# A decoder step on one core: the decode's first queries spread on the chip, its first gathers behind a weight load, weight pages asked for earlier, and two paces of the background work

## The chip, the cores and the metric

One core of one Trainium2 chip runs one program. The metric is the device time of one execution in microseconds (us), the median of several runs. All times within an execution are counted from the first instruction of the profiled execution.

## What is computed

One inference step of a one-layer hybrid decoder for two groups that share all weights: a prompt of 1024 rows and a sample group of 8 sequences with one new row each.

```python
q, k, v, logf, u, z = mixer_inputs(rmsnorm(x, g_mix), w_in, b_f, g_sgu_v)
x = x + concat(rmsnorm(attention), rmsnorm(gated)) @ w_o
x = x + cross_attend(rmsnorm(x, g_cross), mk, mv, w_cq, w_co)
h = rmsnorm(x, g_ffn) @ w_up                  # 5632 columns
f = (silu(conv(gate)) * conv(val)) @ w_down   # causal, width 3
y = rmsnorm(x + f, g_final)
```

The prompt attends causally to its own 1024 rows. Each of the 8 sample rows attends to 64 pages of 128 rows in a paged cache (8 heads of 64, float32), that is 16 MB of keys and 16 MB of values for each sequence, read through a page table. Cross-attention has 256 memory rows; the prompt computes the keys and values, the sample reads them from a cache. Outputs are the final rows of both groups, the new keys and values, and the convolution's states.

## The kernel before

**Two streams of work in one program.** `prompt()` is the main stream. Its phases are, in this order: `p1` (the input projection in four weight blocks of w_in: q, then forget logits and u, then k and v, then z), attention over rows 0 to 511 (`att0`, `attx`), attention over rows 512 to 1023 (`att1`), and then twice, for each half of the rows, `mid` (output projection, cross-attention, its output projection) and `ffn` (44 tiles of w_up in four groups, each followed by its part of w_down). Every large product is made of three float32r matmuls: ACT rounds a weight or activation to a high part (L235, L238), DVE subtracts to get the low part (L236, L239), and PE multiplies (L272, L273, L274).

`sample()` is the background stream: `decode()` (the paged attention of the 8 sequences), then `sample_rest()` (everything after it for the 8 rows).

**How the streams are woven.** Both are generators. Each `yield` of the main stream gives a number, a rough count of PE work. The loop at the end of `build` adds it to an account; when the account reaches `PACE[phase]` it runs one step of the background, takes the pace off the account once for each unit that the step yields, and runs at most `int(t / pace) + 1` steps after one main yield. So a larger pace means fewer background steps in that phase. After `decode()` ends, the pace is `PACE['rest']`, 2.9, in every phase. While `held` is set (the end of each output projection and the norm after it) no step runs, but the account grows; while `paused` is set nothing is added. What is left of the background when the main stream ends runs after it.

The order that results is the program order. A list scheduler in the kernel builder then takes instructions by that order as a priority and by its own simulated times, so an engine's instructions can swap places where that simulation finds an older one not ready.

**decode().** 148 steps, one yield unit each (in attention phases a step with keys is cut into five yields of 0.2). Step g of the first 128 is `kstep` for sequence g // 16, chunk g % 16: an indirect DMA on POOL's queue gathers 1 MB of keys into one of four `kv` buffers (L1428), DVE multiplies them by the query row that is spread over 128 partitions (`qb`; L1444, or L1435 in attention phases) and reduces (L1448, L1436). 18 steps later `vstep` gathers 1 MB of values (L1489), two chunks at every second step, and PE multiplies them by the weights (L1495). The query row of a sequence comes from `prep(b)`: `qs_d`, a DRAM copy that `q_sample` writes (L465), is read back by a broadcasting DMA on SP's queue (L1398). `prep(0)` runs at the start of the first step, `prep(b + 1)` at chunk 14 of sequence b.

**sample_rest().** It normalizes the attention result, then calls `sample_proj` for w_o, w_cq and w_co, with a norm ahead of the next product, cross-attention over the cached memory between w_cq and w_co (8 pages of keys, 8 of values), then 11 double pages of w_up, the gated convolution, and 11 pages of w_down. Each page is 1 MB, goes into the same four `kv` buffers and is asked for on POOL's queue by `page` (L1568). `sample_proj` asks for two pages, yields 2, multiplies them (L331), asks for the next two. After the last norm the old convolution states `stT` are loaded into a `kv` buffer, weighted, and written out as `o_s1` (L1757), one yield.

**PSUM.** `BK()` hands out banks in turn: of three calls one gets a `bb` bank (two of them), two get a `ba` bank (four of them). In the first block of `p1`, `by_rows` holds four banks for tiles 0 to 3 until ACT scales them out (L469), which needs `rstd8` (L412 on POOL).

Of the kernel before, what the change touches and what calls it, by code (L numbers as in the profile page):

```python
# [18 lines left out]
P = 128  # L19
# [53 lines left out]
KS = 2  # L73
BKQ = 1
LA = (2, 2)
PACE = {'p1': 7.0, 'att0': 12.0, 'attx': 26.0, 'mid0': 8.0, 'ffn0': 8.5, 'att1': 11.0, 'mid1': 6.8, 'ffn1': 2.5, 'rest': 2.9}


def build(nc, tc, ctx, a, phases=None):
# [40 lines left out]
    def T2(n=512, dt=F32):  # L120
        return tpool.tile([P, 512], dt, tag="t2", bufs=NT, name=nm("t2"))[:, :n]

    def KV():
        return dpool.tile([P, 2048], F32, tag="kv", bufs=NKV, name=nm("kv"))
# [21 lines left out]
    def BK():  # L146
        turn_[0] += 1
        return BB() if turn_[0] % BR == BR - 1 else BA()
# [225 lines left out]
    def p1(early):  # L374
# [48 lines left out]
        def loaded(c0, n, parts, first=False):  # L423

            sp = [(BK(), off, m) for off, m in parts]
            ws = []
            for kk in range(4):
                if first:
                    load_x(kk, 0)
                w_ = wload(wpair(a["w_in"], kk, c0, n), 2 * n)  # L430
                ws.append(w_)
                if first and kk == 1:
                    constants()
                for ps, off, m in sp:
                    if not first or kk < 2:
                        sample_mm(ps, w_[2], kk, xsT, m, off)
                    elif kk == 3:
                        sample_mm(ps, w_[2], 3, xsT, m, off)
                        with tc.issue_after(newest(ENG.PE)):
                            sample_mm(ps, ws[2][2], 2, xsT, m, off)  # L440
            return ws, [(ps, m) for ps, off, m in sp]
# [20 lines left out]
        def q_sample():  # L462
            sp = sample_sum(*sps[0])
            nc.vector.tensor_scalar(qs, sp, rs8, None, op0=ALU.mult)
            nc.sync.dma_start(qs_d, qs)  # L465

        def evac(ps, dst, sc, tt):
            t = T2()
# [25 lines left out]


        ws, sps = loaded(O_F, 520, [(8, 512), (0, 8)])
        us = T2()[:8]
        fs = sm([8, 8], "fs", 1)
        fl = sm([P, 8, 8], "fl", 1)
# [864 lines left out]

    lastexp = []
    last = {}
    bgs, acc, phase = [], [0.0], ["p1", None]

    def behind(e):
# [4 lines left out]
    def decode():  # L1374
# [14 lines left out]
        for b in range(8):  # L1389
            nc.vector.tensor_tensor(kidx[:, b, :], l16[:, b : b + 1].broadcast_to((P, 16)), io[:, b, :], op=ALU.add)  # L1390
        rmask = const.tile([P, 512], F32, tag="rmask", name="rmask")
        nc.vector.memset(rmask, 1.0)
        nc.vector.memset(rmask.rearrange("p (h k) -> p h k", k=64)[:, :, 0:1], 0.0)
        off = lambda t: bass.IndirectOffsetOnAxis(ap=t, axis=0)

        def prep(b):
            qb = D2()
            nc.sync.dma_start(qb, qs_d[b : b + 1, :].broadcast_to((P, 512)))  # L1398
            s = dpool.tile([P, 512], F32, tag="s", bufs=3, name=nm("s")).rearrange("p (k h) -> p k h", h=8)
            return qb, s  # L1400

# [23 lines left out]
        def kstep(b, ch, st):  # L1425
            qb, s = st
            kv = KV()
            nc.gpsimd.indirect_dma_start(kv, None, a["cache_k"], off(kidx[:, b, ch : ch + 1]))  # L1428
            kvv = kv.rearrange("p (k c) -> p k c", c=512)
            if phase[0][:3] == "att":  # L1430

                for i in range(4):
                    yield 0.2
                    with behind(ENG.DVE):
                        nc.vector.tensor_tensor(kvv[:, i, :], kvv[:, i, :], qb, op=ALU.mult)  # L1435
                        nc.vector.tensor_reduce(  # L1436
                            s[:, ch * 4 + i, :], kvv[:, i, :].rearrange("p (h d) -> p h d", d=64), axis=AX.X, op=ALU.add
                        )
                return 0.2
            sp = KS if phase[0][:3] == "mid" or held[0] else 1  # L1440
            m = 4 // sp
            with behind(ENG.DVE):
                for i in range(0, 4, m):
                    nc.vector.tensor_tensor(  # L1444
                        kvv[:, i : i + m, :], kvv[:, i : i + m, :], qb.unsqueeze(1).broadcast_to((P, m, 512)), op=ALU.mult
                    )
                for i in range(0, 4, m):
                    nc.vector.tensor_reduce(  # L1448
                        s[:, ch * 4 + i : ch * 4 + i + m, :].rearrange("p k h -> p (k h)"),
                        kvv[:, i : i + m, :].rearrange("p k (h d) -> p (k h) d", d=64),  # L1450
                        axis=AX.X,
                        op=ALU.add,
                    )
            return 1
# [110 lines left out]
    def page(dst, src):  # L1565

        with tc.issue_after(rows8[0]) if rows8 else nullcontext():
            nc.gpsimd.dma_start(dst, src)  # L1568
# [24 lines left out]
        for j in range(4):  # L1593
            fin(j // 2, slice(j % 2 * 256, j % 2 * 256 + 256), ps[32 * j : 32 * j + 8, :256])

    def sample_proj(w, xT, fin):
        ps = DV()
        for kk in range(0, 8, 4):
            raws = []
            for k in (kk, kk + 2):  # L1600
                raws.append(KV().rearrange("p (k n) -> p k n", n=D))
                page(raws[-1], w[k * P : (k + 2) * P, :].rearrange("(k p) n -> p k n", p=P))
            yield 2
            for i in range(2):
                with tc.issue_after(newest(ENG.PE)) if i else nullcontext():
                    sample_cols(ps, raws[i], kk + 2 * i, xT, 256)
        yield 1
        quarters(ps, fin)
        yield 1

    def sample_rest():
        yield 1
        xsT = rows_T()
        pn = sm([8, 8], "pn", 1)
# [40 lines left out]
        def add(n, c, ps):  # L1655
            nc.vector.tensor_tensor(xs[n][:, c], ps, xs[n][:, c], op=ALU.add)

        yield from sample_proj(a["w_o"], xsT, add)
        yield from sample_norm(xs, gp[:, G_CROSS : G_CROSS + 8], xsT)
        q2s = pair("s")  # L1660

# [79 lines left out]
        yield 1  # L1741
        sample_T(y, ones[:, 0:8], xsT)
        yield 1
        yield from sample_proj(a["w_co"], xsT, add)
        yield from sample_norm(xs, gp[:, G_FFN : G_FFN + 8], xsT)

        stc = KV()[:, :704].rearrange("p (f c) -> p f c", c=16)
        nc.sync.dma_start(stc, a["stT"])
        s0, s1 = stc[:, :, 0:8], stc[:, :, 8:16]
        wide = lambda c: gp[:, c : c + 44].unsqueeze(2).broadcast_to((P, 44, 8))  # L1750
        v8 = lambda t: t.rearrange("p (f b) -> p f b", b=8)
        sst, tmp = v8(D2(352)), v8(D2(352))
        nc.vector.tensor_tensor(sst, s0, wide(CW), op=ALU.mult)
        nc.vector.tensor_tensor(tmp, s1, wide(CW + 44), op=ALU.mult)
        nc.vector.tensor_tensor(sst, sst, tmp, op=ALU.add)
        nc.vector.tensor_tensor(sst, sst, wide(CB), op=ALU.add)
        nc.sync.dma_start(a["o_s1"], s1)  # L1757
        yield 1
        hs_ = D2(352)
        folds = []  # L1760
        for f4 in range(11):
            ps, rvs = DV(), []
            for q in range(2):
                raw = KV()
                f = f4 * 4 + q * 2
                page(raw.rearrange("p (f d) -> p f d", f=2), a["w_up"][f : f + 2].rearrange("f p d -> p f d"))
                rvs.append(raw.rearrange("p (f k c) -> p k f c", f=2, c=P))
            if folds:
                folds.pop()()
            yield 1  # L1770
            for k in range(8):
                for j in (2, 3, 0, 1):
                    with tc.issue_after(first) if k or j != 2 else nullcontext():
                        mmul(  # L1774
                            ps[32 * j : 32 * j + 32, :P],
                            xsT[:, k, :],
                            rvs[j // 2][:, k, j % 2, :],
                            start=(k == 0),
                            stop=(k == 7),
                            tile_position=(0, 32 * j),  # L1780
                        )
                    if k == 0 and j == 2:
# [13 lines left out]

            folds.append(fold)
# [237 lines left out]
```

## Time and profile before

| what | value |
|---|---|
| runs of the kernel | 1789.9, 1800.49, 1795.0 us; median 1795.0 us |
| the profiled execution: span, first to last instruction | 1791.7 us |
| PE busy | 1735.9 us, 97% |
| DVE busy | 1399.9 us, 78% |
| ACT busy | 733.5 us, 41% |
| POOL busy | 488.3 us, 27% |
| DMA | 521.06 MB, mean 291 GB/s |
| mean granted TensorE clock | 0.993 |

The device time of the profiled execution is not listed beside its span; the span lies 3.3 us below the median of the three runs. A busy share is an average over stages, so the table is only the start: the stages have to be looked at one by one. In the tables by stage that follow, each row has a stretch in us, its length, and then for each engine its busy time in that stretch with the number of instructions in brackets, in the order PE, PEld (weight loads of PE), DVE, ACT, POOL; then the granted clock, the DMA engines' busy share and GB/s. PE's idle time in a stage is the length less the first number.

### The profile page before, as it was taken

How to read it: one execution, taken by the hardware profiler on the slowest of the kernel's cores; microseconds unless marked ns; L12 is line 12 of the kernel's file. 1: busy time of each engine (PE TensorE's matmuls, PEld its weight loads, DVE VectorE, ACT ScalarE, POOL GpSimd, SP SyncE). 2: the span in 40 equal slices, each digit the busy share in tenths (PEclk: the TensorE clock that was granted, in tenths of full speed). 3: DMA queues.
4: the chain of work that ended last, by engine and by line, in shares of the span. 5: the costliest groups of instructions: out<-in, count | busy, mean ns of one | idle time of the engine just before them, and what ended most of it. 6: DMA issues, size and time to landing. Idle time of an engine off the chain costs nothing.

```text
span 1791.7 us, 25124 instructions
## 1 busy us (share of the span) xinstructions
PE 1735.9 (97%) x9653; PEld 1285.7 (72%) x9653; DVE 1399.9 (78%) x1733; ACT 733.5 (41%) x1374; POOL 488.3 (27%) x461
## 2 busy tenths in 40 slices
PE   8999999889999999999999999999999999999997
PEld 5787777655677666767777777766666778768875
DVE  4689658989788986989999999898885549855344
ACT  6332355566643635333333244335353233333232
POOL 1252234443222332333322223433322112102110
PEclk9999999999999999999999999999999999999999
DMA  8786798777697975779788788988879587568982
GB/s 291 297 304 226 294 334 319 259 264 244 254 403 279 363 299 224 282 285 345 290 301 313 291 317 311 376 306 346 320 280 350 214 306 249 191 260 297 359 310 80
DMA packets 157074, 521.06 MB, mean 291 GB/s; under 512 B 20874, under 2 KB 40842, under 8 KB 124186
## 3 DMA queue, kind: packets, MB, share of 16 engines
q0 software_dynamic: 57168, 341.14, 50.0%
q1 hardware_dynamic: 92874, 165.73, 26.5%
q10 hardware_dynamic: 6912, 12.59, 1.9%
q8 instruction: 76, 1.25, 0.3%
q14 instruction: 44, 0.36, 0.1%
HBM read 495.47 MB, written 23.93 MB: 290 GB/s over the span
## 4 chain that ended last, share of the span: by engine, by line
PE 53%; issue 9%; DMA 8%; DVE 6%; ACT 2%; POOL 2%; POOLq 0%; DVEq 0%; ACTq 0%; SPq 0%
DMA kv<-cache_v,io 6%; PE ba L272 6%; PE ba L274 6%; PE ba L273 6%; PE dv L1495 4%; PE bb L272 3%; PE bb L273 3%; PE bb L274 3%; PE ba L1063 1%; DVE s L1448 1%; PE ba L1064 1%; PE ba L1065 1%; PE dv L331 1%; DMA kv<-cache_k,io 1%; PE dv L1774 1%
## 5 line engine op out<-in xcount | busy, mean ns | idle before, releaser
L235 ACT ACTIVATE wh<-wr 128x1024 fp32r<-128x1024 f32 (+2 forms) x220 | 228.6, 1044 | 443.3 <-PE ba L273 142.3
L236 DVE TENSOR_TENSOR wl<-wr,wh 128x1024 fp32r<-128x1024 f32 (+2 forms) x220 | 262.7, 1200 | 165.1 <-PE ba L274 57.4
L1428 POOL DMA_INDIRECT kv<-cache_k,io x128 | 186.9, 1460 | 606.8 <-DVE s L1448 327.2
L1444 DVE TENSOR_TENSOR kv<-kv,d 128x1024 f32<-128x1024 f32 (+1 forms) x156 | 258.0, 1681 | 32.6 <-DMA kv<-cache_k,io 32.6
L1448 DVE TENSOR_REDUCE s<-kv 128x16 f32<-128x1024 f32 (+1 forms) x156 | 258.4, 1672 | 0.0
L1489 POOL DMA_INDIRECT kv<-cache_v,io x128 | 160.8, 1256 | 239.4 <-PE dv L1495 155.2
L272 PE MATMUL ba<-u,wh 128*128 128x512 f32 x528 | 209.3, 397 | 0.0
L274 PE MATMUL ba<-u,wl 128*128 128x512 f32 x528 | 209.0, 396 | 0.0
L273 PE MATMUL ba<-u,wh 128*128 128x512 f32 x528 | 208.5, 395 | 0.5 <-DVE u L239 0.5
L272 PE MATMUL ba<-wh,u 128*128 128x512 f32 (+1 forms) x495 | 186.1, 379 | 0.9 <-ACT u L235 0.9
L273 PE MATMUL ba<-wl,u 128*128 128x512 f32 (+1 forms) x495 | 185.1, 375 | 1.3 <-DVE wl L236 1.3
L274 PE MATMUL ba<-wh,u 128*128 128x512 f32 (+1 forms) x495 | 183.4, 375 | 0.0
L1495 PE MATMUL dv<-kv,s 128*32 128x512 f32 x1024 | 127.1, 598 | 1.6 <-DMA kv<-cache_v,io 1.6
L274 PEld LDWEIGHTS ba<-u,wl 128*128 128x128 f32 x528 | 99.2, 188 | 29.0 <-issue 6.5
L272 PEld LDWEIGHTS ba<-u,wh 128*128 128x128 f32 x528 | 99.3, 188 | 26.4 <-issue 4.8
L273 PEld LDWEIGHTS ba<-u,wh 128*128 128x128 f32 x528 | 99.2, 188 | 25.2 <-issue 2.3
L272 PEld LDWEIGHTS ba<-wh,u 128*128 128x128 f32 x495 | 93.0, 188 | 25.0 <-issue 6.5
L272 PE MATMUL bb<-u,wh 128*128 128x512 f32 x272 | 108.7, 400 | 0.0
L274 PE MATMUL bb<-u,wl 128*128 128x512 f32 x272 | 108.0, 398 | 0.0
L273 PE MATMUL bb<-u,wh 128*128 128x512 f32 x272 | 107.9, 397 | 0.0
L273 PEld LDWEIGHTS ba<-wl,u 128*128 128x128 f32 x495 | 93.0, 188 | 20.1 <-DVE wl L236 1.9
L274 PEld LDWEIGHTS ba<-wh,u 128*128 128x128 f32 x495 | 92.9, 188 | 19.5 <-issue 1.6
(454 smaller groups left out, 3310.6 us busy)
## 6 DMA issues: line engine op xcount, KB each, us to landing
wr<-w_up SPq DMA_DIRECT2D x88, 512.0 KB
kv<-w_up POOLq DMA_DIRECT2D x22, 1024.0 KB
wr<-w_down SPq DMA_DIRECT2D x40, 512.0 KB
kv<-w_down POOLq DMA_DIRECT2D x11, 1024.0 KB
wr<-w_in SPq DMA_DIRECT2D x16, 512.0 KB
wr<-w_o SPq DMA_DIRECT2D x16, 512.0 KB
wr<-w_cq SPq DMA_DIRECT2D x16, 512.0 KB
wr<-w_co SPq DMA_DIRECT2D x16, 512.0 KB
```

The costliest lines, as they stand in the source:

```text
L235: nc.scalar.activation(h, src, AF.Copy)
L236: nc.vector.tensor_tensor(l, src, h.bitcast(F32), op=ALU.subtract)
L272: mmul(out, sh, mh, start=(i == 0), stop=False)
L273: mmul(out, sh, ml, start=False, stop=False)
L274: mmul(out, sl, mh, start=False, stop=(i == n - 1))
L331: mmul(ps[32 * j : 32 * j + 32, :w], xT[:, k, :] if nk == 8 else xT[:, k * 8 : k * 8 + 32], raw[:, q, j * w : (j + 1) * w], start=(k == 0) ...
L1063: mmul(pss[i], mh[k][:, tb], wh, start=(k == korder[0]), stop=False)
L1428: nc.gpsimd.indirect_dma_start(kv, None, a["cache_k"], off(kidx[:, b, ch : ch + 1]))
L1444: nc.vector.tensor_tensor(kvv[:, i : i + m, :], kvv[:, i : i + m, :], qb.unsqueeze(1).broadcast_to((P, m, 512)), op=ALU.mult)
L1448: nc.vector.tensor_reduce(s[:, ch * 4 + i : ch * 4 + i + m, :].rearrange("p k h -> p (k h)"), kvv[:, i : i + m, :].rearrange("p k (h d) -> ...
L1489: nc.gpsimd.indirect_dma_start(kv, None, a["cache_v"], off(kidx[:, b, ch : ch + 1]))
L1495: mmul(dv[32 * j : 32 * j + 32, :], s[:, ch * 4 : ch * 4 + 4, :].rearrange("p k h -> p (k h)"), kvv[:, j, :], start=(ch == 1), stop=(ch == ...
```

## The change

Five edits:

1. The first sequence's query rows are spread over the partitions by a matmul of a selecting matrix (`one`: row 0 is ones, the other seven rows zeros) with `qs`, right after `qs` is made in `q_sample`, and copied from PSUM to a `d2` buffer by DVE. `prep(0)` uses that buffer; the broadcasting read of `qs_d` remains for the other seven sequences. `q_sample` also sets `paused`, which is cleared when the second weight block's loads and sample products have been written down.
2. A one-element copy on POOL from the fourth raw weight tile of the second block into the first `kv` buffer stands ahead of the first gather, so the gather waits for that weight tile to land.
3. `sample_proj` asks for all four pages at its start, or takes them from a list `ready`; `then`, if given, asks for two pages of the next matrix after each two products. w_o's call asks for w_cq's pages, w_co's call for the first four of w_up.
4. The `stT` block moves to the start of `sample_rest`, in two halves with `t2` and `d2` buffers; its result is kept in the buffer of `rmask`, which the decode no longer needs. One yield of one unit goes.
5. `PACE['att1']` goes from 11 to 16 and `PACE['mid1']` from 6.8 to 7.6.

```diff
-PACE = {..., 'att1': 11.0, 'mid1': 6.8, 'ffn1': 2.5, 'rest': 2.9}
+PACE = {..., 'att1': 16.0, 'mid1': 7.6, 'ffn1': 2.5, 'rest': 2.9}
...
             nc.sync.dma_start(qs_d, qs)
+            one = T2(P)[:8]
+            nc.vector.tensor_copy(one, ident[:8, 0:1].broadcast_to((8, P)))
+            ps = BK()
+            mmul(ps[:, :512], one, qs, start=True, stop=True)
+            q0.append(D2())
+            nc.vector.tensor_copy(q0[0], ps[:, :512])
+            paused[0] = True
...
         ws, sps = loaded(O_F, 520, [(8, 512), (0, 8)])
+        landed.append(ws[3][2])
+        paused[0] = False
...
         def prep(b):
-            qb = D2()
-            nc.sync.dma_start(qb, qs_d[b : b + 1, :].broadcast_to((P, 512)))
+            qb = D2() if b else q0[0]
+            if b:
+                nc.sync.dma_start(qb, qs_d[b : b + 1, :].broadcast_to((P, 512)))
...
             kv = KV()
+            if landed:
+                nc.gpsimd.tensor_copy(kv[0:1, 0:1], landed.pop()[0:1, 0, 0:1])
             nc.gpsimd.indirect_dma_start(kv, None, a["cache_k"], off(kidx[:, b, ch : ch + 1]))
...
-    def sample_proj(w, xT, fin):
+    def sample_proj(w, xT, fin, then=None):
         ps = DV()
+        own = [ready.pop(0) for _ in range(4)] if ready else [rows_of(w, k) for k in range(0, 8, 2)]
         for kk in range(0, 8, 4):
-            raws = []
-            for k in (kk, kk + 2):
-                raws.append(KV().rearrange("p (k n) -> p k n", n=D))
-                page(raws[-1], w[k * P : (k + 2) * P, :].rearrange("(k p) n -> p k n", p=P))
+            raws = own[kk // 2 : kk // 2 + 2]
             yield 2
...
+            if then:
+                ready.extend(then(kk + i) for i in (0, 2))
...
     def sample_rest():
+        sst = v8(idle[0][:, :352])
+        for f0 in (0, 22):
+            fs = slice(f0, f0 + 22)
+            stc = T2(352).rearrange("p (f c) -> p f c", c=16)
+            nc.sync.dma_start(stc, a["stT"][:, fs, :])
+            s0, s1 = stc[:, :, 0:8], stc[:, :, 8:16]
+            tmp = v8(D2(176))
...
+            nc.sync.dma_start(a["o_s1"][:, fs, :], s1)
         yield 1
...
-        yield from sample_proj(a["w_o"], xsT, add)
+        yield from sample_proj(a["w_o"], xsT, add, partial(rows_of, a["w_cq"]))
...
-        yield from sample_proj(a["w_co"], xsT, add)
+        yield from sample_proj(a["w_co"], xsT, add, up_of)
...
-                raw = KV()
-                f = f4 * 4 + q * 2
-                page(raw.rearrange("p (f d) -> p f d", f=2), a["w_up"][f : f + 2].rearrange("f p d -> p f d"))
+                raw = ready.pop(0) if ready else up_of(f4 * 4 + q * 2)
```

More of the change, by code (lines that the diff above doesn't have):

```diff
@@ L75 @@
 LA = (2, 2)
-PACE = {'p1': 7.0, 'att0': 12.0, 'attx': 26.0, 'mid0': 8.0, 'ffn0': 8.5, 'att1': 11.0, 'mid1': 6.8, 'ffn1': 2.5, 'rest': 2.9}
+PACE = {'p1': 7.0, 'att0': 12.0, 'attx': 26.0, 'mid0': 8.0, 'ffn0': 8.5, 'att1': 16.0, 'mid1': 7.6, 'ffn1': 2.5, 'rest': 2.9}
 def build(nc, tc, ctx, a, phases=None):
@@ L1366, in build @@
     last = {}
+    q0, landed, idle = [], [], []
     bgs, acc, phase = [], [0.0], ["p1", None]
@@ L1391, in decode @@
         rmask = const.tile([P, 512], F32, tag="rmask", name="rmask")
+        idle.append(rmask)
         nc.vector.memset(rmask, 1.0)
@@ L1594, in quarters, with rows_of, up_of @@
             fin(j // 2, slice(j % 2 * 256, j % 2 * 256 + 256), ps[32 * j : 32 * j + 8, :256])
-    def sample_proj(w, xT, fin):
+    ready = []
+    def rows_of(w, k):
+        raw = KV().rearrange("p (k n) -> p k n", n=D)
+        page(raw, w[k * P : (k + 2) * P, :].rearrange("(k p) n -> p k n", p=P))
+        return raw
+    def up_of(f):
+        raw = KV()
+        page(raw.rearrange("p (f d) -> p f d", f=2), a["w_up"][f : f + 2].rearrange("f p d -> p f d"))
+        return raw
+    def sample_proj(w, xT, fin, then=None):
         ps = DV()
+        own = [ready.pop(0) for _ in range(4)] if ready else [rows_of(w, k) for k in range(0, 8, 2)]
         for kk in range(0, 8, 4):
-            raws = []
-            for k in (kk, kk + 2):
-                raws.append(KV().rearrange("p (k n) -> p k n", n=D))
-                page(raws[-1], w[k * P : (k + 2) * P, :].rearrange("(k p) n -> p k n", p=P))
+            raws = own[kk // 2 : kk // 2 + 2]
             yield 2
@@ L1611, in sample_rest @@
     def sample_rest():
+        wide = lambda c, f0=0, f1=44: gp[:, c + f0 : c + f1].unsqueeze(2).broadcast_to((P, f1 - f0, 8))
+        v8 = lambda t: t.rearrange("p (f b) -> p f b", b=8)
+        sst = v8(idle[0][:, :352])
[5 more added lines that the diff above has]
+            tmp = v8(D2(176))
+            nc.vector.tensor_tensor(sst[:, fs, :], s0, wide(CW, f0, f0 + 22), op=ALU.mult)
+            nc.vector.tensor_tensor(tmp, s1, wide(CW + 44, f0, f0 + 22), op=ALU.mult)
+            nc.vector.tensor_tensor(sst[:, fs, :], sst[:, fs, :], tmp, op=ALU.add)
+            nc.vector.tensor_tensor(sst[:, fs, :], sst[:, fs, :], wide(CB, f0, f0 + 22), op=ALU.add)
+            nc.sync.dma_start(a["o_s1"][:, fs, :], s1)
         yield 1
@@ L1743, in sample_rest @@
         yield 1
-        yield from sample_proj(a["w_co"], xsT, add)
+        yield from sample_proj(a["w_co"], xsT, add, up_of)
         yield from sample_norm(xs, gp[:, G_FFN : G_FFN + 8], xsT)
[L1747 to L1758, printed above, removed]
         hs_ = D2(352)
```

## The prediction

> **What bounds the kernel now.** I read the page's first part, then the table by stages, then who waits for whom inside the stages that the change touches, then single instructions. Page and table:
>
> ```profile
> span 1791.7 us, 25124 instructions
> PE 1735.9 (97%) x9653; PEld 1285.7 (72%) x9653; DVE 1399.9 (78%) x1733; ACT 733.5 (41%) x1374; POOL 488.3 (27%) x461
> ```
> ```profile
> 55.00:68.00 13.00, 10.15 (x73) 6.77 (x72) 5.11 (x4) 6.45 (x9) 0.00 (x0) 1.00 0.75 264
> 280.00:395.00 115.00, 103.50 (x618) 74.76 (x617) 98.39 (x186) 64.63 (x159) 51.34 (x70) 0.94 0.81 285
> 395.00:505.00 110.00, 101.47 (x707) 70.74 (x704) 97.97 (x156) 68.20 (x133) 28.47 (x35) 1.00 0.78 278
> 720.00:1100.00 380.00, 378.69 (x1780) 283.16 (x1783) 358.46 (x333) 133.09 (x202) 107.79 (x78) 1.00 0.81 302
> 1100.00:1340.00 240.00, 231.43 (x1181) 165.53 (x1170) 210.43 (x248) 106.03 (x224) 84.69 (x64) 1.00 0.88 334
> 1340.00:1395.00 55.00, 55.00 (x297) 35.49 (x297) 28.29 (x41) 19.99 (x32) 13.30 (x14) 1.00 0.88 323
> 1395.00:1762.00 367.00, 366.08 (x2512) 275.63 (x2512) 214.03 (x314) 118.71 (x208) 54.74 (x80) 1.00 0.73 265
> ```
>
> PE works in 97% of the span; 1791.7 - 1735.9 = 55.8 us are idle. The change removes no matmul, so it can win only idle time. The rows say where that lies: 2.9 us around 55:68 (the second weight block), 11.5 in the first attention, 8.5 in the second, 8.6 in 1100:1340 (the second `mid`). From 1340 to 1762, where the sample's pages stream, PE has no idle time: pages that arrive earlier there win nothing directly.
>
> The end:
>
> ```profile
> 1760.69 0.62 PE L331 MATMUL dv<-kv,d 128*32 128x256 f32 x4
> 1767.06 0.31 SPq L1828 DMA_DIRECT2D o_ys<-vsum  x1
> 1782.00 0.40 PE L274 MATMUL bb<-wh,u 128*128 128x512 f32 x1
> 1785.49 1.42 DVE L1361 SCALAR_TENSOR_TENSOR u<-u,rn3r,u 128x512 f32<-128x512 f32 x2 [0.66 <-POOL rn3r L223]
> ```
>
> The sample's last product ends at 1761.3, the prompt's at 1782.4. The background has 21.1 us of slack, and the prompt sets the end.
>
> **Part 1, the start of the decode.**
>
> ```profile
> PE bb L306 <- DMA wr<-w_in: 1.6, 2, 1.2
> PE ba L273 <- DVE wl L236: 1.3, 3, 0.7
> SPq L1398 <- DMA qs_d<-t: 23.3, 1, 23.3
> 36.35 1.17 POOL L1428 DMA_INDIRECT kv<-cache_k,io  x1 [22.49 <-DMA kv<-x]
> 28.64 6.47 SPq L249 DMA_DIRECT2D wr<-w_in  x4
> 28.77 1.02 PE L323 MATMUL ba<-t,cp 128*8 128x512 f32 x2
> 32.47 0.73 DVE L464 TENSOR_SCALAR t<-ba,rs 8x512 f32<-8x512 f32 x1
> 35.18 0.40 PE L272 MATMUL ba<-wh,u 128*128 128x512 f32 x1
> 35.41 0.39 PE L273 MATMUL ba<-wl,u 128*128 128x512 f32 x1
> 40.65 0.67 ACT L469 ACTIVATE t<-bb,rstd 128x512 f32<-128x512 f32 x1
> 39.26 2.04 POOL L412 TENSOR_TENSOR rstd<-xv,mhalf 128x4 f32<-128x4 f32 x2
> ```
>
> The second block's weights are issued from 28.6 on; gathers join at 36.4, and PE then waits 1.6 us for weights and 1.3 us for their low parts. With the gathers behind the fourth weight tile this stall goes: **-2.9** (ends: 0, if x and the weights alone fill the DMA; -2.9). SP's 23.3 us block goes too, but SP is early everywhere, so I price it at nothing. The product adds PE work like the L323 matmul of 512 columns, 1.02 us: **+1.0**. It needs L464, which ended at 33.2; the builder's order can put other matmuls ahead of it, and if it does not, PE waits up to 33.2 - 29.8 = 3.4 us (ends 0 to 3.4, taken 0). DVE's two added copies, 0.7 us at most each by L464, stand in a stretch where DVE is mostly idle.
>
> Two bounds here count for the range. The added `BK()` turns the banks by one: tile 4, which began at 35.18 in a free `ba` bank, now draws a `bb` bank that is held until the scaling at 40.65. That is 0 to 5.5 us; I take 0, since two `ba` banks stay free for tiles 5 and 6 and the builder can take those first. And POOL's one-element copy waits for a weight: behind it in POOL's queue stand all gathers and, if the builder put it first, the powers L412 that release the four banks. In program order the powers come first and were done at 41.3, so I take 0 (end: about 10 us, from 39.3 to some 50).
>
> **Part 2, the thinner decode.** The steps are counted from the yields. `paused` takes the yields of `by_rows` from the third on and of four tiles, about 36 units, at pace 7 five steps. `att1` yields 74.6 units: 6.8 steps at pace 11, 4.7 at 16. `mid1` yields 160.4: 23.6 at 6.8, 21.1 at 7.6. Walking the loop through with the remainders of the account: p1 26 to 21, att1 8 to 5, mid1 25 to 23. Ten of the 148 steps move into the last ffn, which gets 28 instead of 18.
>
> ```profile
> L1436 DVE TENSOR_REDUCE s<-kv 128x8 f32<-128x512 f32 x31 | 20.1, 675 | 0.1
> L1435 DVE TENSOR_TENSOR kv<-kv,d 128x512 f32<-128x512 f32 x29 | 19.6, 690 | 0.1
> PE ba L807 <- ACT wr L817: 2.9, 6, 0.8
> PE bb L836 <- ACT u L843: 2.4, 7, 0.8
> ```
>
> These are rows of 395:505: the decode costs DVE 4 x (0.675 + 0.690) = 5.5 us a step in attention. DVE is busy 98 of 110 us there, and its maxima come ahead of ACT's exponentials (L817), for which PE waits. Three steps less take 16 us, DVE falls to about 75%. PE's idle time of 8.5 us is half explained by waits that queue behind DVE, so I take half of it: **-4** (ends 0 and -8.5). In `mid1` two steps of 25 go; its idle time lies mainly around norms while `held` is set, when no step runs anyway: **-0.5** (ends 0 and -2). The 0.94 clock of the first attention is left as it is: `att0` and `attx` keep their seven steps.
>
> **Part 3, where the ten steps land.**
>
> ```profile
> L1428 POOL DMA_INDIRECT kv<-cache_k,io x128: 932/1010/6296, 36.4 to 1308.6; - x128
> L1489 POOL DMA_INDIRECT kv<-cache_v,io x128: 932/950/4861, 169.7 to 1389.8; - x128
> L1495 PE MATMUL dv<-kv,s 128*32 128x512 f32 x1024 | 127.1, 598 | 1.6 <-DMA kv<-cache_v,io 1.6
> L1495 PE MATMUL dv<-kv,s 128*32 128x512 f32 x116 | 14.1, 599 | 0.0
> ```
>
> Before, keys end at 1308.6, ahead of the last ffn, whose start moves values alone. After, 8 key and 26 value pages, 34 MB, fall into its first tiles. A tile is 24 matmuls that start 0.23 us apart (35.18 and 35.41 above), 5.5 us, and a value page costs PE 127.1 / 128 = 1.0 us: 11 tiles and 26 pages are 86 us, in which 34 + 5.5 MB would have to move, 460 GB/s. The busiest stretches quoted here and below move 320 to 350. At 350 it takes 113 us, so the decode ends some 27 us behind its place. DVE has room (28 of 55 us). PE need not wait: in 1340:1395 the gathers were also at the DMA's rate, and PE idled 0.0 us, as the builder lets main tiles pass. **0** (ends 0 and 12: half the lag).
>
> **Part 4, the end of the sample.** Before, from the start of the last ffn: 18 steps at 2.5 take 44 units and the rest takes 101 x 2.9 = 294, together 338 of the 361 units of that ffn: slack 23, which the trace shows as 21.1 us. After: 28 steps take 70, the rest (one yield less) 291, sum 361: **slack nothing**. The last two pages are multiplied right after the prompt's last product, if DMA keeps up.
>
> ```profile
> 1335.00:1395.00 60.00, 60.00 (x325) 39.70 (x326) 31.25 (x49) 22.24 (x39) 13.30 (x14) 1.00 0.81 297
> 1395.00:1450.00 55.00, 55.00 (x308) 39.86 (x308) 30.60 (x52) 15.91 (x27) 6.85 (x10) 1.00 0.54 197
> 1450.00:1570.00 120.00, 119.08 (x578) 92.02 (x577) 93.57 (x123) 41.48 (x64) 20.15 (x32) 1.00 0.73 258
> 1570.00:1620.00 50.00, 50.00 (x278) 34.76 (x277) 27.73 (x46) 18.90 (x32) 4.43 (x6) 1.00 0.63 226
> 1620.00:1700.00 80.00, 80.00 (x851) 64.19 (x850) 33.20 (x47) 22.80 (x46) 15.46 (x22) 1.00 0.92 350
> 1745.00:1783.00 38.00, 37.40 (x192) 27.96 (x191) 19.34 (x36) 10.09 (x24) 2.20 (x5) 1.00 0.21 74
> ```
>
> Ten key and value steps bring some 16 MB more. Against 350 GB/s, there is room for 8.4 MB in 1395:1450, 11.0 in 1450:1570, 6.2 in 1570:1620 and 10.5 after 1745. Two of these holes are chains of norms, and that is where edit 3 asks for pages ahead. So the lag of 27 us can be worked off, and the bytes just fit. The sample's own chain from its last product to its last issue took 1767.06 - 1761.3 = 5.8 us, the prompt's 1786.9 - 1782.4 = 4.5. With slack nothing, one more product of 0.6 and a last page some 2 us late: 0.6 + 2 + 1.3 = **+4** (ends 0 and 25: the whole lag left).
>
> Edit 4 halves four DVE operations and doubles two small DMAs, in stretches where PE is full and DVE is not: nothing.
>
> **Sum.** -2.9 + 1.0 - 4 - 0.5 + 0 + 4 = -2.4, so a span of 1789.3. The median is 3.3 above the span before, so **1793 us**: no change that can be told. A measurement of this kernel tells about 0.5% from no change, below 1786.0 or above 1804.0.
>
> **The rivals.** (a) *The sample ends late.* This is the slower one. Mechanism: the 27 us of lag are not worked off, because each norm chain restarts later and the two holes stay. It decides once the last w_down page lands over some 12 us after the prompt's last product; from there every us counts. With 15 to 25 us left instead of 2, 1793 + 13 to 23: about 1811. For it: slack nothing, the 1620:1700 row already at 350. Against: 36 MB of room for 16. Chance 0.24.
>
> (b) *Attention is freed by more than half.* If DVE alone holds the second attention, 7 of 8.5 us go, `mid1` gives 2, and the tail costs nothing: 1795 - 2.9 + 1.0 - 7 - 2 = 1784. For it: DVE 98 of 110. Against: both waits name ACT. Chance 0.16.
>
> (c) *The clock.* In 280:395 the granted clock was 0.94, which costs up to 115 x 0.06 = 6.9 us, elsewhere 1.00. If the shifted decode fills PE's pauses there, 1793 - 7 = 1786, and just below with a little of (b); the same mechanism can cost as much if new pauses form. [...] Chance 0.10.
>
> (d) *It does not do what it says.* The stall at 55:68 stays because x and the weights fill the DMA alone (1795 + 1 - 4.5 + 4 = 1796). Chance 0.12, inside "same".
>
> **Chances and range.** The forecast has 0.38. Faster by over 0.5%: (b) and most of (c), with the forecast's lower edge, 0.27. Slower: (a) and the unknown costs of parts 1 and 3, 0.26. Same: 0.47. The lower bound, 1778, is (b) and (c) together, the upper, 1812, is (a).
>
> **What would show it.** Right: PE idle under 0.5 us around 55:68; idle in the second attention near 4 us; the last w_down page asked for beside the prompt's last tiles; PE full through the last ffn. Wrong: PE waiting for L469 or the product before 45 us; L1495 waiting for `cache_v` in the last ffn; an end made of L331, L1656, L1827.

## The result, and the profile after

The changed kernel took 1837.7 us (median; 1835.6 to 1838.3), the kernel before 1795.7 us beside it: 1.0223 times as long, 95% interval 1.0203 to 1.0244. It is slower by 42 us, where I had forecast 1793 with a range up to 1812.

First the page of the changed kernel, span and busy time:

```profile
span 1836.2 us, 25136 instructions
PE 1752.7 (95%) x9655; PEld 1295.0 (71%) x9655; DVE 1396.4 (76%) x1721; ACT 735.7 (40%) x1375; POOL 497.9 (27%) x462
```

PE is idle for 83.5 us of the span, before it was 55.8. Its busy time grew by 16.8 us with only two matmuls more, so matmuls also ran slower (mean granted clock 0.981, before 0.993). The table by stages, with the columns as before, the last row being the new tail:

```profile
55.00:68.00 13.00, 13.00 (x106) 10.72 (x105) 7.49 (x6) 7.50 (x10) 0.13 (x1) 1.00 1.02 409
280.00:395.00 115.00, 99.42 (x598) 69.14 (x598) 92.35 (x175) 63.23 (x155) 44.22 (x60) 0.97 0.78 263
395.00:505.00 110.00, 99.84 (x681) 69.71 (x679) 83.32 (x132) 66.67 (x131) 21.46 (x28) 0.97 0.66 222
1340.00:1482.00 142.00, 141.44 (x717) 99.52 (x717) 104.61 (x122) 48.14 (x75) 37.38 (x31) 1.00 0.82 297
1395.00:1762.00 367.00, 365.63 (x2178) 269.28 (x2177) 231.76 (x337) 122.43 (x205) 65.25 (x84) 1.00 0.75 274
1482.00:1762.00 280.00, 278.63 (x1735) 210.81 (x1734) 176.35 (x265) 95.27 (x166) 43.20 (x65) 1.00 0.71 259
1783.00:1826.00 43.00, 25.32 (x308) 12.00 (x306) 4.42 (x10) 2.23 (x8) 8.41 (x12) 0.67 0.90 343
```

The stall at 55:68 is gone (13.00 busy of 13). In the second attention DVE fell from 98 to 83 us, and PE's idle time rose from 8.5 to 10.2. The new tail of 43 us holds 25.3 us of PE work, 17.7 us of idle time and a clock of 0.67. The attentions and the first `mid` got worse as well. These two rows, the kernel before and then the changed one, lie between the same two products of the prompt (the 320th and the 480th of its L272 matmuls, own counting):

```profile
239.00:712.00 473.00, 447.41 (x2549) 326.96 (x2548) 395.96 (x600) 254.47 (x550) 153.05 (x166) 0.98 0.80 294
233.00:720.00 487.00, 448.91 (x2513) 328.17 (x2512) 382.00 (x576) 253.29 (x549) 148.30 (x163) 0.97 0.76 272
```

PE idles 25.6 us there before and 38.1 us after. The timeline of the end, changed kernel (start, length, instruction, idle before it and its releaser):

```profile
1782.84 0.39 PE L274 MATMUL ba<-wh,u 128*128 128x512 f32 x1
...
1792.15 3.64 PE L1802 MATMUL dv<-kv,xg 128*32 128x128 f32 x64 [6.17 <-DMA kv<-w_up]
...
1826.30 0.84 DVE L1698 TENSOR_TENSOR dec<-dv,dec 8x256 f32<-8x256 f32 x2 [27.50 <-PE dv L331]
...
1831.39 0.29 SPq L1856 DMA_DIRECT2D o_ys<-vsum  x1
```

The prompt ends at 1783.2, 0.8 us after its place in the kernel before (1782.4), although all work of this tail has left its stretch. The sample then still has a last page of w_up to wait for and all of w_down. The view of the page buffers, changed kernel (count; then shortest, middle and longest length in ns; first and last start in us), says how late the sample is:

```profile
L1442 POOL DMA_INDIRECT kv<-cache_k,io x128: 934/946/7808, 48.4 to 1396.5; - x128
L1503 POOL DMA_INDIRECT kv<-cache_v,io x128: 936/954/6428, 191.1 to 1482.6; - x128
...
L1582 POOL DMA_DIRECT2D kv<-w_down x11: 716/716/734, 1785.5 to 1815.3; - x11
```

The last value gather came 92.8 us later than before (1389.8), the last page of w_down 71.0 us later; in the kernel before the view has:

```profile
L1568 POOL DMA_DIRECT2D kv<-w_down x11: 713/713/716, 1703.0 to 1744.3; - x11
```

The waits of POOL from 1340 to 1490 and of PE from 1762 on, changed kernel (total, times, longest):

```profile
POOL kv L1503 <- PE dv L1509: 65.6, 12, 14.3
POOL kv L1442 <- DVE s L1462: 30.8, 6, 9.5
```
```profile
PE dv L331 <- DMA kv<-w_down: 8.4, 8, 2.4
PE dv L1802 <- DMA kv<-w_up: 6.2, 1, 6.2
```

While the decode should catch up, its gathers wait for a free one of the four `kv` buffers: for PE's value products (L1509) and DVE's reductions (L1462). At the end PE waits for pages.

### The profile page after: what moved, and what is told of

Same layout as the page of the kernel before. It is cut to its first block, busy times and chain, and to the rows that moved or that the text cites. A ratio compares the mean times of both kernels' runs of the same rounds, so it can differ in the third digit from the quotient of the medians.

```text
span 1836.2 us, 25136 instructions
## 1 busy us (share of the span) xinstructions
PE 1752.7 (95%) x9655; PEld 1295.0 (71%) x9655; DVE 1396.4 (76%) x1721; ACT 735.7 (40%) x1375; POOL 497.9 (27%) x462
## 3 DMA queue, kind: packets, MB, share of 16 engines
q8 instruction: 76, 1.25, 0.3%
## 4 chain that ended last, share of the span: by engine, by line
PE 54%; issue 8%; DMA 5%; DVE 4%; ACT 2%; POOL 1%; POOLq 0%; DVEq 0%; ACTq 0%
PE ba L272 8%; PE ba L273 8%; PE ba L274 8%; PE dv L1509 5%; PE bb L272 4%; PE bb L273 4%; PE bb L274 4%; DMA kv<-w_up 2%; PE ba L1074 1%; PE ba L1073 1%; PE ba L1072 1%; DMA kv<-w_down 1%; PE dv L331 1%; PE ba L1090 1%; PE ba L1091 1%
## 5 line engine op out<-in xcount | busy, mean ns | idle before, releaser
L1458 DVE TENSOR_TENSOR kv<-kv,d 128x1024 f32<-128x1024 f32 (+1 forms) x159 | 265.1, 1694 | 25.9 <-DMA kv<-cache_k,io 25.6
L1462 DVE TENSOR_REDUCE s<-kv 128x16 f32<-128x1024 f32 (+1 forms) x159 | 265.4, 1688 | 0.2
L1503 POOL DMA_INDIRECT kv<-cache_v,io x128 | 177.4, 1386 | 276.4 <-PE dv L1509 206.4
L272 PE MATMUL ba<-u,wh 128*128 128x512 f32 x544 | 216.2, 398 | 0.0
L273 PE MATMUL ba<-u,wh 128*128 128x512 f32 x544 | 215.2, 396 | 0.0
L274 PE MATMUL ba<-u,wl 128*128 128x512 f32 x544 | 214.7, 396 | 0.0
L272 PE MATMUL ba<-wh,u 128*128 128x512 f32 (+1 forms) x487 | 185.0, 382 | 0.9 <-ACT t L823 0.5
L1509 PE MATMUL dv<-kv,s 128*32 128x512 f32 x1024 | 125.2, 598 | 1.5 <-DMA kv<-cache_v,io 1.5
L272 PEld LDWEIGHTS ba<-u,wh 128*128 128x128 f32 x544 | 102.3, 188 | 32.4 <-issue 9.0
L273 PEld LDWEIGHTS ba<-u,wh 128*128 128x128 f32 x544 | 102.2, 188 | 31.6 <-issue 9.4
L272 PEld LDWEIGHTS ba<-wh,u 128*128 128x128 f32 x487 | 92.3, 190 | 23.7 <-issue 5.5
L272 PE MATMUL bb<-u,wh 128*128 128x512 f32 x256 | 101.2, 395 | 0.0
L274 PE MATMUL bb<-u,wl 128*128 128x512 f32 x256 | 101.0, 394 | 0.0
L273 PE MATMUL bb<-u,wh 128*128 128x512 f32 x256 | 100.9, 394 | 0.0
```

Source lines behind the costliest of these rows:

```text
L272: mmul(out, sh, mh, start=(i == 0), stop=False)
L273: mmul(out, sh, ml, start=False, stop=False)
L274: mmul(out, sl, mh, start=False, stop=(i == n - 1))
L1458: nc.vector.tensor_tensor(kvv[:, i : i + m, :], kvv[:, i : i + m, :], qb.unsqueeze(1).broadcast_to((P, m, 512)), op=ALU.mult)
L1462: nc.vector.tensor_reduce(s[:, ch * 4 + i : ch * 4 + i + m, :].rearrange("p k h -> p (k h)"), kvv[:, i : i + m, :].rearrange("p k (h d) -> ...
L1503: nc.gpsimd.indirect_dma_start(kv, None, a["cache_v"], off(kidx[:, b, ch : ch + 1]))
```

## The experiments

I began with rival (a), that the sample merely ends late, against a cost in the prompt. Ratios are to the kernel before, run beside each kernel, with 95% intervals. Every kernel computes everything.

**The edits in groups.** `e1_paces_back` is the change without edit 5, `e2_paces_only` the kernel before with edit 5 alone.

```diff
-PACE = {..., 'att1': 16.0, 'mid1': 7.6, ...}
+PACE = {..., 'att1': 11.0, 'mid1': 6.8, ...}
```

> The changed kernel with the old paces (att1 11, mid1 6.8): edits 1 to 4 without edit 5. Theory L (lateness: what counts is only how many decode steps are pushed into the last ffn, whichever edit pushes them; 10 steps cost 21 us of slack and 43 us of tail, 6.4 us a step; five of them are the start's): tail about 11 us late, 1800 us. Rival P (the thinner paces alone cost, since the start's pause hides behind the weight load): 1790. Rival S (the pages asked for ahead hold the four kv buffers and delay the sample): stays near 1835.

> The kernel before with the new paces alone (edit 5). Theory L: some five steps late, 32 us less 21 of slack, about 1805. Rival P: 1835. Both expect the prompt's own last product no earlier than before. Rival S: 1795 or less, with less idle time of TensorE in the second attention.

`e3_start_only` has edits 1 and 2, `e4_sample_only` edits 3 and 4, both with the old paces.

> The kernel before with edits 1 and 2 alone (first queries by a product, first gather behind the weight tile, decode paused until then). Theory L: the weight stall of 2.9 us goes, five steps are late, they eat the slack and some more: 1795 to 1805. Rival P: 1792, sample still done before the prompt. A third theory, that the pause alone is the cause: 1830.

> The kernel before with edits 3 and 4 alone (pages asked for ahead, convolution states early). Theories L and P: the prompt sets the end, 1795 within 4 us, and the sample's last product up to 10 us earlier against the prompt's. Rival S: slower, 1805 or more.

| kernel | us | ratio |
|---|---|---|
| e1, edits 1 to 4 | 1844.0 | 1.0295 (1.0265 to 1.0324) |
| e2, edit 5 | 1810.2 | 1.0087 (1.0060 to 1.0114) |
| e3, edits 1 and 2 | 1841.5 | 1.0276 (1.0242 to 1.0309) |
| e4, edits 3 and 4 | 1789.7 | 0.9986 (0.9972 to 1.0001) |

The late sample falls as the whole cause. In e1 its last page is asked for 25 us before the prompt ends (1829.7), there is no tail, and the time is no better than that of the changed kernel:

```profile
L1582 POOL DMA_DIRECT2D kv<-w_down x11: 713/713/716, 1760.6 to 1804.1; - x11
```

The start of the decode carries the cost, and the sample's edits cost nothing. The costs do not add: edit 5 costs 17 us alone, but on top of edits 1 to 4 it takes a little back (1.0223 with it, 1.0295 without). Edit 5 alone leaves this in the second attention, e2:

```profile
395.00:505.00 110.00, 102.28 (x693) 72.17 (x690) 84.22 (x134) 67.11 (x132) 26.29 (x32) 0.95 0.66 227
```

DVE is as thin there as in the changed kernel, yet PE idles 7.7 us (8.5 before), and the clock is 0.95 in place of 1.00.

**What of the start.** `e5_start_same_turn` takes the product's bank from the other pool, so that the turn of the banks stays; `e6_turn_only` only turns the banks; `e7_pause_only` only pauses; `e8_sample_product` is e4 with the product and no pause or wait.

```diff
# e5, against e3
-            ps = BK()
+            ps = BA()
# e6, against before, in q_sample
+            turn_[0] += 1
# e7, against before
+            paused[0] = True
...
+        paused[0] = False
```

> Edits 1 and 2 on the kernel before, but the product's bank is taken from the ba banks directly, without a turn of BK, so every later bank of the program falls as before. Theory M (alignment: five late decode steps put other decode work beside the attention and the norms): about 1840 as with the turn. Rival B (the added turn shifts bb and ba through the whole program, and matmuls wait for banks): 1793, decode five steps late and the sample still ending before the prompt.

> The kernel before with one more turn of BK at the place of the product and nothing else: no instruction added, no pause, no wait. Theory M: 1795 within 5. Rival B: about 1840, with TensorE waiting in the norms and projections after the attentions.

> The kernel before with the pause of the background alone (from the third step of the first block to the second block's loads); the first queries still come by the broadcasting read, no wait, no added turn. Theory M: about 1840, keys of sequence 3 gathered some 70 us later as with edits 1 and 2. Rival B: 1795.

> Edits 3 and 4 with the product of edit 1 from a ba bank without a turn of BK, and neither pause nor wait: the decode on time. Theory M and rival B alike: within 4 us of edits 3 and 4 alone, 1790; the synchronizing queue no longer blocked for 23 us at the start, the weight stall of some 3 us still there, since gathers still join at 36 us.

e5 1847.6 us, 1.0324 (1.0297 to 1.0351); e6 1802.0, 1.0056 (1.0035 to 1.0078); e7 1844.6, 1.0311 (1.0280 to 1.0342); e8 1800.9, 1.0054 (1.0035 to 1.0074). Two lines that issue nothing cost all of it. The pause drops five decode steps by the end of `p1`. The bank turn alone costs some 9 us, though e5, without it, is no faster than e3. In e8 the product in place of the first broadcasting read, without turn, pause or wait, costs some 8 us (1800.9 beside 1793.3), where I had expected nothing: its ratio is clear of those of edits 3 and 4 alone (e4 above, e16 below).

**Late, or paused, or only moved?** e9 has no pause and a slower `p1`, which by the count of the yields places every step from the end of `p1` on where the pause put it. e10 pauses and makes the steps up by a faster `p1`, e11 does so for edits 1 to 4, e12b only makes `p1` faster.

```diff
-PACE = {'p1': 7.0, ...}
+PACE = {'p1': 8.73, ...}    # e9; 5.69 with the pause in e10 and e11; 6.4 in e12b
```

> The kernel before with nothing changed but the pace of the phase p1, 8.73 in place of 7.0, and no pause. Counted from the yields, this places every decode step from the end of p1 on exactly where the pause alone placed it (162 of 162 gathers), with 21 steps in p1 in place of 26. If the lateness of the five steps is what costs: about 1844 us as with the pause alone (1835 to 1850), with some 10 or more half-clock windows. If the pause itself costs, as a gap in the decode at the second weight block: about 1796 us.

> The kernel before with the pause alone, and the pace of p1 at 5.69, so that the steps lost in the pause are made up by the end of p1; after that 101 of 162 gathers stand where they stood before, the others within a unit or two. If lateness costs: about 1795 us (1790 to 1805). If the pause costs in another way than by lateness: about 1844 us as with the pause alone.

> Edits 1 to 4 of the change with the old paces of the second attention and mid, and p1 at 5.69 to make up the pause. If lateness costs: the sum of the sample edits (1790 us) and of the product with its turn of the banks (+6 to +11): 1790 to 1802 us. If the start of the decode costs in another way: about 1842 us, as with the old paces alone.

> The kernel before with the pace of p1 at 6.4: three steps earlier by the end of p1 (29 in place of 26), nothing else. If being late is what costs, being early costs nothing or wins a little: 1785 to 1797 us. If any shift against a hand-set placement costs, by new pauses of the matrix engine and half-clock windows behind them: 1805 to 1840 us.

e9 1847.3 us, 1.0294 (1.0270 to 1.0318); e10 1812.1, 1.0093 (1.0068 to 1.0119); e11 1809.1, 1.0078 (1.0053 to 1.0102); e12b 1837.5, 1.0236 (1.0209 to 1.0263). The pause costs by where it puts the decode, as e9 shows, and two thirds of it are undone when the steps are made up; e10 and e11 still miss the ranges that I had expected if lateness were all. That lateness is what costs falls too: three steps *early* cost 2.4%. The attentions of e9, in the table by stages:

```profile
280.00:395.00 115.00, 99.42 (x586) 70.01 (x584) 89.26 (x169) 60.56 (x151) 40.62 (x57) 0.94 0.72 243
395.00:505.00 110.00, 92.63 (x604) 62.84 (x604) 86.76 (x141) 58.05 (x120) 28.20 (x36) 0.89 0.66 221
```

Idle time is 15.6 and 17.4 us there (11.5 and 8.5 before), and the clock falls to 0.89 in the second, with less work on DVE than before.

**One step, none, and the tail.** e13 makes every step from the end of `p1` on one place late, e14 issues none in the attentions (they come later), e15 speeds up the sample's rest in the changed kernel, e16 is e4 again.

```diff
# e13, against before
+PACE = {'p1': 7.3, ...}
# e14, against before, in the loop that weaves the streams
-        if paused[0]:
+        if paused[0] or phase[0][:3] == "att":
# e15, against after
+PACE = {..., 'rest': 2.4}
```

> The kernel before with the pace of p1 at 7.3: 25 steps by its end in place of 26, one late, nothing else. If the cost grows with the lateness (five steps cost some 50 us): about 10 us, 1800 to 1808. If any displacement costs: 1810 to 1845, like three steps early or five late. If single steps are free: 1790 to 1797.

> The kernel before, but the two attentions issue no decode steps; the fourteen steps that stood there come later, so the whole time means little and the stages are read. If the decode steps in the attentions make the pauses (before, 11.5 us idle in the first attention and 8.5 in the second): idle of 0 to 4 us in each and no half-clock window there. If the pauses are the attentions' own and the steps fill them: idle of 10 us or more in each, with more half-clock windows than before.

> The changed kernel with the pace of the sample's rest at 2.4 in place of 2.9, which by the yields ends the sample some 50 units earlier. If the tail of 43 us is made of pauses and half clock beside 25 us of work that has to be done anyway: 1808 to 1822 us, the prompt's last product moving from 1783 to about 1800. If the sample is limited by its own transfers and cannot go faster: 1830 to 1840 with the tail still there.

> Edits 3 and 4 alone once more, in five rounds, as the candidate that beats the kernel before: it stood at 1789.7 us, 0.9986 with an interval up to 1.0001. If the gain is real: a ratio of 0.996 to 0.9995. If it was a matter of the run: an interval around 1.

e13 1830.7 us, 1.0211 (1.0182 to 1.0239): being late by one step of 148 costs 37 us. e15 1836.1, 1.0245 (1.0216 to 1.0275): no gain in time. e16 1792.6, 0.9998 (0.9982 to 1.0014): no version beats the kernel before. e14 was run once, 1848.9 us; its stages:

```profile
280.00:395.00 115.00, 104.11 (x640) 77.27 (x639) 67.45 (x129) 69.99 (x173) 28.60 (x49) 0.99 0.47 145
395.00:505.00 110.00, 104.44 (x653) 75.41 (x652) 73.20 (x101) 63.04 (x126) 19.60 (x23) 0.98 0.57 201
```

With no step in the attentions 16.5 us of idle time stay in the two stretches together, of 20.0 before; in the second alone it is 5.6 of 8.5. The clock is higher in the first stretch (0.99 for 0.94), lower in the second (0.98 for 1.00). This lies between my two expectations: in this one run most of the pauses are the attention's own, and the steps of the kernel before add little to them. And the pages of e15, beside those of the changed kernel:

```profile
L1503 POOL DMA_INDIRECT kv<-cache_v,io x128: 932/962/6427, 191.0 to 1479.6; - x128
...
L1582 POOL DMA_DIRECT2D kv<-w_down x11: 713/713/713, 1782.6 to 1807.4; - x11
```

From the last value gather to the last page of w_down it took 327.8 us at a pace of 2.4, and 332.7 at 2.9 (1482.6 to 1815.3). So the sample's rest takes some 330 us at both paces. But e15's unchanged time says less than it seems to. Its last matmul ends at 1817.3, 8.9 us earlier than in the changed kernel; what then holds the end is ACT's order (e15, timelines of DVE and ACT):

```profile
1750.45 0.69 DVE L1024 TENSOR_TENSOR u<-bb,u 128x512 f32<-128x512 f32 x1 [3.42 <-PE bb L274]
...
1780.31 0.69 DVE L1024 TENSOR_TENSOR u<-ba,u 128x512 f32<-128x512 f32 x1 [2.78 <-PE ba L274]
...
1818.22 0.63 ACT L230 ACTIVATE junk<-dec 8x512 bf16<-8x512 f32 x1 [29.91 <-DVE dec L1698]
...
1819.92 0.63 ACT L230 ACTIVATE junk<-u 128x512 bf16<-128x512 f32 x1
...
1825.20 0.63 ACT L230 ACTIVATE junk<-u 128x512 bf16<-128x512 f32 x1
```

The prompt's last sums (`u`) are there from 1750 to 1781, but ACT squares them for the last norms only after the sample's own squares (`junk<-dec`), for which it waits 29.9 us. So a faster pace did end the sample earlier; a new wait in the prompt took the gain back.

**The builder's order, or the steps themselves?** A moved step also changes the order that the builder gives to the prompt's own work: of the prompt's matmul records in the trace, told apart by line, tiles and shape, 98% stand in e4 at the place in the list that they have in the kernel before, in e13 79%, in e9 72% (own counting). e17 is e13 and e18 is e9 with ties of issue order between the prompt's own instructions, engine by engine.

```diff
+        for d in steps:          # the list of the kernel before, by place in program order
+            k += d
+            i = mains[e][k]
+            if before is not None:
+                tc.add_manual_dep(i, before.name, ...NoSync...)
+            before = i
```

> The decode one step late (p1 at 7.3), and the prompt's own instructions tied, engine by engine, into the order in which they stand in the kernel before. If the builder's new order of the prompt is what costs: 1788 to 1802 us, in place of 1831, with half-clock windows as few as before (some 17 us in all). If the displaced steps collide with the prompt where they stand: 1820 to 1840, as without the tie. Between 1802 and 1820 both have a part.

> The decode five steps late (p1 at 8.73, which costs what the pause costs), and the prompt's own instructions tied into the order of the kernel before, but for a fiftieth of each engine's list (from 26 to 28%), which does not go together with the late steps. If the builder's new order is what costs: 1790 to 1810 us in place of 1847. If the displaced steps collide where they stand: 1835 to 1855. Between, both have a part.

e17 1828.5 us, 1.0175 (1.0141 to 1.0209); e18 1848.4, 1.0292 (1.0260 to 1.0323). The prompt's own order is not the cause. By the same counting 99.9% of the prompt's matmuls in e17 stand in their old place, and it still loses 31 us:

```profile
280.00:395.00 115.00, 101.29 (x582) 72.12 (x581) 92.74 (x175) 60.07 (x152) 39.95 (x57) 0.93 0.72 249
395.00:505.00 110.00, 93.17 (x634) 63.06 (x633) 87.65 (x141) 62.32 (x126) 31.41 (x42) 0.94 0.72 236
```

Three of its pauses in the two attentions, from the timeline of PE:

```profile
335.29 1.11 PE L838 MATMUL ms<-cp,t 128*128 128x128 f32 x4 [2.26 <-DVE dec L1422]
...
379.24 0.66 PE L838 MATMUL ms<-cp,t 128*128 128x128 f32 x4 [0.72 <-DVE m L1473]
...
397.32 0.44 PE L838 MATMUL ms<-cp,wr 128*128 128x128 f32 x2 [1.95 <-DVE s L1485]
```

Once a sequence the decode's softmax passes through the `ms` bank, and here the attention's transposes draw that bank behind it: one place where a moved step collides. These three make 4.9 us. The kernel before has the same kind of wait in the attentions, 3.1 us in all, so it explains little of the 18 us that e17 loses up to the end of the second attention (the last of L874's matmuls ends at 511.0, L872's before at 492.6); the rest is spread over many waits of 0.5 to 4 us for ACT and DVE, and over the lower clock.

**What all kernels have in common.** The time until the last matmul splits into PE's idle time, half of the time that the clock records show at half speed, and a remainder (own counting from the traces, us; the fourth column has the whole time at half speed, of which half is taken off). The half is an estimate of what is lost there: the prompt's 128x512 matmuls of the changed kernel start 0.43 us apart from 276.33 to 277.61, at a clock of 0.50, and 0.23 us apart from 278.98 to 279.90, at 1.00.

| kernel | last matmul ends | idle | at half clock | remainder |
|---|---|---|---|---|
| e4 | 1776.9 | 45.8 | 6.8 | 1727.6 |
| before | 1782.4 | 46.5 | 17.1 | 1727.4 |
| e6 | 1796.5 | 55.3 | 23.9 | 1729.2 |
| e2 | 1803.5 | 54.6 | 47.8 | 1725.0 |
| e10 | 1807.3 | 59.9 | 34.1 | 1730.4 |
| e13 | 1820.8 | 69.3 | 51.2 | 1725.9 |
| after | 1826.2 | 73.6 | 59.4 | 1723.0 |
| e3 | 1830.0 | 76.7 | 51.2 | 1727.7 |
| e18 | 1835.5 | 76.2 | 71.7 | 1723.5 |
| e9 | 1837.2 | 78.1 | 71.7 | 1723.3 |

The remainder is 1723 to 1730 while the end moves by 60 us. PE's work is the same within a few us in all; what differs is pauses and the time at half clock, and in the traces the half clock comes behind the pauses. The clock records change in steps of 3.41 us: up to the last matmul of the kernel before, the four stretches at half clock are 3.41, 3.41, 6.83 and 3.41 us long. I took all windows of that length at full clock, from 60 us on, in the traces of all 20 profiled kernels and counted which were followed by one at half:

| PE idle in the window, us | windows | followed by half clock |
|---|---|---|
| under 1.3 | 9706 | 0 |
| 1.3 to 1.6 | 87 | 10 |
| 1.6 to 2.0 | 73 | 48 |
| 2.0 and more | 114 | 114 |

## Why the prediction was wrong, point by point

- **Part 1** was right at the place where it made a sum: the stall is gone, and the product took 1.12 us (two matmuls, at 36.28) for 1.0 forecast; PE does not wait for it. Over the whole run the same product costs some 8 us (e8). What failed most is what was left out of it: the pause was treated as a count of five steps that move to the last ffn. Where the steps in between then stand had no price, and that was the largest cost: the pause alone, with the old paces, costs 51 us (e7).
- **Part 2** failed. DVE did fall (98 to 83 us), but PE's idle time in the second attention went from 8.5 to 10.2 us instead of to 4; with edit 5 alone it is 7.7 (e2), a gain of 0.8 for 4. The step "half explained by waits that queue behind DVE, so I take half of it" failed: without any step in the attentions 5.6 of the 8.5 us stay there (e14). As a whole edit 5 alone costs 17 us.
- **Part 3** had the pages nearly right (6 keys and 26 values after 1340, for 8 and 26) and the rate wrong: 297 GB/s in 1340:1482 instead of 350, while POOL's gathers waited 96 us of 1340:1490 for a free buffer. The decode ended at 1482.6, not at 1340 + 113 = 1453: it lay 57 us behind its place (1340 + 86 = 1426), not 27. PE indeed did not wait: 365.6 us busy of 367, and the sign against it, value products waiting for `cache_v` in the last ffn, is absent.
- **Part 4**, "so the lag of 27 us can be worked off", was about right in what can be worked off and failed because the lag was twice as long. From the last value gather to the last w_down page it took 332.7 us, before 354.5 (1389.8 to 1744.3): some 20 us were won, where 25 were forecast (27 less the 2 us in the sum), though the DMA moved 259 GB/s after the decode, below the 350 that I had filled the holes with. The end is made of L331 and L1698, the sign that I had named for rival (a): the last w_down page was asked for 32 us after the prompt's last product. For the changed kernel its mechanism and place were right, its price (13 to 23 us) was half of the tail's 43. That its time comes nearest to the measured one is in part luck: e1, which has no tail, takes no less time.
- **Rival (c)** named the right currency and had it the wrong way round as the likelier case. What ties the clock to the pauses here is the count above: half clock behind 114 of 114 windows with 2.0 us of idle time or more, behind none of 9706 with under 1.3. The tail has 17.7 us of idle time and loses up to 14 us by the clock (0.67 over 43 us). The rest lies ahead of it: with this work pushed behind the prompt (25 us as it ran there; by the split above some 15 us at full clock, a remainder of 1711.9 up to the prompt's end in place of 1727.4), the prompt still ended 0.8 us later, with some 9 us more of idle time and 14 us more at half clock than before. Most of that arises in the attentions and the first `mid`: 38.1 us of idle time there in place of 25.6 for the same products of the prompt.
- So this was not one term of the right sum with a wrong size: the sum had no term for where the moved steps stand. With the old paces the loss shows as a late prompt (e1), with the thinner paces as a late sample; in both it is idle time and clock.

What stays open is which instruction lengthens which pause, and why a turn of the banks or the product, which move no step, cost 8 to 9 us too. The `ms` bank is one case, seen in e17; the others weren't tried one by one. That the cost grows so fast because of the step in the counts above (half clock behind 0 of 9706 windows with under 1.3 us of idle time, behind 114 of 114 with 2.0 or more) is inferred from them and was not tried by itself.

## What to carry to other kernels

A stream that is woven into another by counted paces can't be priced by its counts: a shift by one step of 148 to a later place cost 2.1%, by three to an earlier place 2.4%. All shifts tried here lost, none won, so the paces of the kernel before may simply stand at a lucky or a well tuned place; no run here shows which. Before changing how many background steps a phase gets, ask whether all later steps keep their places, and if not, make the count up before the attentions begin, which here saved two thirds of the loss (e10). Look at the sum of the matrix engine's pauses within a window of the clock records, not at each one's length alone: in the changed kernel the window from 387.8, with 2.09 us idle in pauses of at most 1.21, was followed by half clock, the one from 1183.1, with a single pause of 1.25, was not.

## What the runs showed of the hardware

- In the traces of the 20 profiled kernels, a window of 3.41 us in which PE was idle for 2.0 us or more was followed by half clock in 114 of 114 cases, with 1.3 to 2.0 us in 58 of 160, with under 1.3 us in 0 of 9706.
- At a clock of 0.50 the 128x512 matmuls started 0.43 us apart, at 1.00 0.23 us (changed kernel, around 277 and 279 us). From this I estimate that a window of 3.41 us at half clock costs up to half its length, 1.7 us, beside the pause itself. In e13, 34 us more at half clock (51.2 and 17.1) make 17, by this estimate, of the 38 us that its last matmul ends later, and 23 us more of idle time the rest.
